# Hybrid encoder layer: a head's outputs spread over more steps with one power for both halves, and the down projection's loads issued one at a time

## The chip, the cores and the metric

The kernel runs on one core of a Trainium2 chip. The metric is the device time of one execution in microseconds (us); of several runs the median counts. Inputs and outputs are float32. The engines are called as in the profile: PE (TensorE, matrix products), PEld (its weight loads), DVE (VectorE), ACT (ScalarE), POOL (GpSimd) and SP (SyncE, which here only issues DMA transfers). Each engine works through its own queue strictly in order; an instruction that waits holds up all that stand behind it on that engine.

## What is computed

One layer on x of 1024 positions by 1024 channels:

```python
h = rmsnorm(x, attn_norm_w)
proj = h @ w_in                      # 1024 x 8192, split into the parts below
glu_in, q, v, z_f, z_b, og, g_a, g_b = split(proj)
a = pointwise(silu(layernorm(dwconv31(glu(glu_in)))))
o = scan(q, v, z_f) + scan_reversed(q, v, z_b)        # 8 heads of 128 columns, chunks
of = o * rsqrt(mean(o * o, axis=-1) + EPS)            # per head, over its 128 columns
bmix = (of * norm_w * silu(og)) @ o_w
x = x + (sigmoid(g_a) * a + sigmoid(g_b) * bmix) @ w_out
h2 = rmsnorm(x, ffn_norm_w)
x = x + (silu(dwconv3(h2 @ w_gate)) * (h2 @ w_up)) @ w_down   # 2816 hidden columns
return rmsnorm(x, final_norm_w)
```

The change touches two places: the line `of = ...` with the multiplication by `silu(og)`, and the product with `w_down`.

## The kernel before

Activations are kept transposed, with channels on the 128 partitions and positions along the row. The 1024 positions are two halves of 512, and a page is a tile of 128 x 512 float32. Each big product is made of three passes over numbers split into a high and a low part: `mm3` issues the matmuls of lines 143, 144 and 145 (128 x 512 each). A split is a cast on ACT (`split`, line 121) and a subtraction on DVE (`split_lo`, line 118); the results are called `hx` or `gx` for activations and `wp` or `wq` for weights.

The order of PE's instructions is the order in which the code issues them. For DVE, ACT, POOL and SP a scheduler orders the instructions when the program is built, by dependencies, by the place in the code and by when it believes that a buffer is free; so a line that stands later in the code may come earlier on such an engine.

To weave two pieces of work on PE, the code writes them as generators. A `Stream` wraps one; `fill(n)` advances it by n steps (fractions are owed, and a negative amount is paid back first), `drain()` runs it out. A step of a job made by `std_job` is two k-blocks, that is six matmuls.

The stage of the heads (about 540 to 990 us) has three pieces of work on PE. `dense` is the rest of the input projection, plain big products. The main loop runs over 8 heads and, inside, two halves: `scan_levels` yields four times (levels 8, 16, 32, 64; products of line 838, for level 8 also line 851; the values v are transposed on line 1034 in the third), then `scan_states` yields three times (two transposes of kG on line 894, each copied by ACT on line 896 into kT, then the products of line 903, whose results go to the states Sf and Sb on lines 909, 911 and 921). After each of these seven steps `between` fills `dense` by 1.3, advances the base of the next half by two steps (DVE work: DE, Qh, Kh, qF, kG, lines 730, 733, 786), and advances `pending` by one. `pending` holds the outputs of the head before. Thus a head's outputs are worked off while the next head's first half is scanned.

`outputs` first finishes Sb (line 989), yields, and hands over to `scan_outputs`. There, before the change, each half in turn is: 11 small matmuls into the bank ob (line 942); a copy into a tm page (944); four squares with a sum over 128 columns each (948); on POOL a scaling and a power of the four sums (`rstd_small`, lines 404 and 405), which gives `ors`; four scalings of the page on ACT (955); a yield. Then for each half: four transposes into a tr bank (963), the product with the norm weight and the gate page (965), and a store to `d_bm`; for the last head a split into `hx` takes the place of the store. The gates are loaded from `d_og` (line 114) into tm pages. There are four tm pages in all, shared with the loads of v and of `d_bm`, two tr banks, one ob bank and three mm banks. Behind the last head `bm_loads` reads `d_bm` back and splits it for the product with `o_w`.

The down projection (from about 1617 us) runs over five groups of 4, 4, 5, 5 and 4 blocks of hidden columns. `load_g` loads the pages of a group from `d_g` (line 1239, three ev pages in turn) and splits them. The pages of the next group are asked for when the current group's stream has made three steps. The result of the first group is copied from the mm bank by ACT (`first_evac`, line 1244, into `xr`), that of the others added on DVE (line 1250).

Of the kernel before, what the change touches and what calls it, by code (L numbers as in the profile page):

```python
# [10 lines left out]
F32 = mybir.dt.float32  # L11
# [3 lines left out]
AF = mybir.ActivationFunctionType  # L15
# [3 lines left out]
P = 128  # L19
# [12 lines left out]
DK = 128  # L32
# [12 lines left out]
def tile_hybrid_encoder(  # L45
# [22 lines left out]
    nc = tc.nc  # L68
    PSUM = bass.MemoryType.PSUM
    V, A, G, T = nc.vector, nc.scalar, nc.gpsimd, nc.tensor  # L70
# [12 lines left out]
    cp = ctx.enter_context(tc.tile_pool(name="const", bufs=1))  # L83
# [7 lines left out]
    def nm(s):  # L91
        uid[0] += 1
        return f"{s}_{uid[0]}"
# [3 lines left out]
    def bank(tag):  # L97
        return ps.tile([P, H], F32, tag=tag, name=nm(tag), bufs=BANKS[tag])

    def page(pool, tag, bufs, dt=F32):  # L100
        return pool.tile([P, H], dt, tag=tag, name=nm(tag), bufs=bufs)

    def tmp():
        return page(mp, "tm", 4)

    def ev():
        return page(mp, "ev", 3)

    def hx():
        return page(mp, "hx", 32, F32R)  # L110

    def load(src):
        t = tmp()
        nc.sync.dma_start(t, src)
        return t
# [4 lines left out]
    def split(hi, lo, src, eng):  # L120
        A.copy(hi, src)  # L121
        split_lo(eng, lo, src, hi)
        return hi, lo
# [25 lines left out]
    def run_jobs(jobs, lead=0, prime=0):  # L149


        jobs = jobs if isinstance(jobs, collections.deque) else collections.deque(jobs)
        ready = collections.deque()

        def prepare(n):
            while jobs and len(ready) < n:
                prep, run = jobs.popleft()
                ready.append((run, prep()))

        prepare(max(prime, 1))  # L160
        if prime:
            yield
        while ready:
            run, w = ready.popleft()
            pieces = run(w)
            for _ in itertools.islice(pieces, lead):
                yield
            prepare(1)
            yield from pieces
            prepare(1)  # L170
# [199 lines left out]
    def vec(key, i):  # L370
        name, o = vec_off[key]
        return vecs[name][:, o + i : o + i + 1]


    def scratch(name, *dims):
        if not dims:
            return dp.tile([P, H], F32, name=name)
        return [scratch(f"{name}_{i}", *dims[1:]) for i in range(dims[0])]
# [8 lines left out]
    d_og = scratch("d_og", NH, 2)  # L387
# [15 lines left out]
    def rstd_small(dst, ss, n):  # L403
        G.tensor_scalar(dst, ss, 1.0 / n, EPS, op0=ALU.mult, op1=ALU.add)
        G.tensor_tensor(dst, dst, mhalf.to_broadcast(list(dst.shape)), op=ALU.pow)
# [257 lines left out]
    for half in range(2):  # L663
# [18 lines left out]
        rs = next(rstd)  # L682
# [32 lines left out]
    dense = Stream(run_jobs(rest_jobs))  # L715


    hp = tc.alloc_tile_pool(name="heads", bufs=1, reuse_waits="tile")
# [207 lines left out]
    def scan_outputs(h, kept, Sf, Sb):  # L926


        ons, gates = [], [load(d_og[h][half]) for half in range(2)]
        for half in range(2):  # L930
            S_t, v, qF = kept[half]
            o = bank("ob")
            for c in range(4):
                sl = slice(c * P, (c + 1) * P)
                g = half * 4 + c
                terms = [(S_t[:, c, :], v[:, c, :])]
                if g > 0:
                    terms.append((qF[:, 1, sl], Sf[half][:, c, :]))
                if g < 7:
                    terms.append((qF[:, 0, sl], Sb[half][:, c, :]))  # L940
                for n, (l, r) in enumerate(terms):
                    T.matmul(o[:, sl], l, r, start=(n == 0), stop=(n == len(terms) - 1))
            on = tmp()
            A.copy(on, o)
            ss = cp.tile([P, 4], F32, name=nm("oss"), tag="oss", bufs=2)
            for c in range(4):
                junk = hp.tile([P, DK], F32, tag="jk", name=nm("jk"), bufs=1)
                A.activation(
                    junk, on[:, c * P : (c + 1) * P], AF.Square, accum_out=ss[:, c : c + 1]
                )  # L950
            rs = cp.tile([P, 4], F32, name=nm("ors"), tag="ors", bufs=2)
            rstd_small(rs, ss, DK)
            for c in range(4):
                sl = slice(c * P, (c + 1) * P)
                A.activation(on[:, sl], on[:, sl], AF.Copy, scale=rs[:, c : c + 1])
            ons.append(on)
            yield
        for half in range(2):
            if half:
                yield  # L960
            b = bank("tr")
            for c in range(4):
                T.transpose(b[:, c * P : (c + 1) * P], ons[half][:, c * P : (c + 1) * P], ident)
            bt = ev()
            V.scalar_tensor_tensor(bt, b, vec("hn", h), gates[half], op0=ALU.mult, op1=ALU.mult)
            if h == NH - 1:
                bm[h][half] = split(hx(), hx(), bt, V)
            else:
                nc.sync.dma_start(d_bm[h][half], bt)
            yield  # L970
# [14 lines left out]
    def outputs(h, kept, Tt, Sf, Sb):  # L985
        for c in range(5, -1, -1):
            hf, cc = c // 4, c % 4
            n1, c1 = (c + 1) // 4, (c + 1) % 4
            V.scalar_tensor_tensor(
                Sb[hf][:, cc, :],  # L990
                Sb[n1][:, c1, :],
                Tt[:, n1, 1, c1 : c1 + 1],
                Sb[hf][:, cc, :],
                op0=ALU.mult,
                op1=ALU.add,
            )
        yield
        yield from scan_outputs(h, kept, Sf, Sb)
# [3 lines left out]
    def bm_loads(half):  # L1002
        for h in range(NH - 1):
            bm[h][half] = split(hx(), hx(), load(d_bm[h][half]), V)
# [5 lines left out]
    pending = Stream(iter(()))  # L1010
    for h in range(NH):
# [31 lines left out]
        pending = Stream(outputs(h, kept, Tt, Sf, Sb))  # L1043
# [2 lines left out]
    pending.fill(1)  # L1046
    dense.fill(left - 20)
    pending.fill(1)
    dense.fill(6)
    pending.fill(1)  # L1050
    dense.fill(6)
    bm_loads(0)
    pending.fill(1)
    dense.fill(8)
# [173 lines left out]
    def g_page():  # L1228
        return hx() if next(n_g) == 0 else page(fd, "gx", 16, F32R)

    groups = [4, 4, 5, 5, 4]
    gs, jobs = [], []

    def load_g(f0, n):
        for f in range(f0, f0 + n):
            gs.append([])
            for half in range(2):
                t = ev()
                nc.sync.dma_start(t, d_g[f][half])
                gs[-1].append(split(g_page(), g_page(), t, V))  # L1240
# [13 lines left out]
    def down_jobs(f0, n, halves, evac):  # L1254
        return [
            std_job(
                w_cols(ffn_w_down, f0 * P, n, i * P),
                n,
                lambda k, half: gs[f0 + k][half],
                evac(i),  # L1260
                halves,
            )
            for i in range(ND)
        ]
# [39 lines left out]
    def finish(half):  # L1304
        turn_out(ND - 1, half)
        ss, y = out_sum[half], out_y[half]
        rs = cp.tile([P, 4], F32, name=nm("frs"), tag="frs", bufs=2)
        V.tensor_reduce(rs, ss.rearrange("p i c -> p c i"), axis=AX.X, op=ALU.add)
        rstd_small(rs, rs, D)
        for c in range(4):  # L1310
            if c % 2:
                A.activation(y[:, c, :], y[:, c, :], AF.Copy, scale=rs[:, c : c + 1])
            else:
                V.tensor_scalar(y[:, c, :], y[:, c, :], rs[:, c : c + 1], None, op0=ALU.mult)
            n = half * 4 + c
            nc.sync.dma_start(out[0, n * P : (n + 1) * P, :], y[:, c, :])
# [4 lines left out]
    f0 = 0  # L1321
# [4 lines left out]
    for n, group in enumerate(groups):  # L1326
        last = n == len(groups) - 1
        for hs in ((0,), (1,)) if last else ((0, 1),):
            st = Stream(run_jobs(down_jobs(f0, group, hs, final_evac if last else add_evac if n else first_evac)))
            st.fill(3)  # L1330
            while late:
                finish(late.pop())
            if not last:
                load_g(f0 + group, groups[n + 1])
            st.drain()
        f0 += group
    finish(late.pop())
# [33 lines left out]
```

## Time and profile before

| what | us |
|---|---|
| median of 3 runs | 1888.44 |
| lowest and highest run | 1885.39, 1894.96 |
| the profiled execution | 1889.98 |
| its span, first to last instruction | 1888.20 |
| busy in the span: PE, DVE, ACT, POOL | 1790.4, 1270.7, 797.8, 212.4 |
| mean granted TensorE clock | 0.982 |

The profile is of one execution. Busy time says how long an engine had at least one instruction at work. In a timeline row the first number is the start in us from the span's beginning, the second the duration, then engine, line, operation, output and input tiles, shape and count; brackets hold the time that the engine stood idle before it and what ended that. In a row of waits the first name waited for the second: total us, number of times, longest. In a row of a stretch the columns are its length, the busy time of PE, PEld, DVE, ACT and POOL with counts, the granted TensorE clock (1.00 is full), the busy share of the DMA engines and GB/s.

### The profile page before, as it was taken

To read this page: it belongs to the slowest core of one execution; us is meant where nothing else is said; L and a number is where in the kernel's file an instruction comes from. 1 tells how busy PE (TensorE), PEld (TensorE's weight loads), DVE (VectorE), ACT (ScalarE), POOL (GpSimd) and SP (SyncE) were. 2 spreads that over 40 slices of the span, in tenths; PEclk is the share of its full clock that TensorE was granted. 3 is DMA by queue.
4 is the path that set the end of the run, shared out by engine and by line. 5 is a ranking of instruction groups with operands and counts; after the bars stand their busy time and mean duration, and the time that the engine had idled before them with its cause. 6 is when DMAs were issued, how large, how long until landed. Compare 5 with 4: busy or idle time off the path is not lost. (4 is left out here: it accounts for less than half of the span.)

```text
span 1888.2 us, 23731 instructions
## 1 busy us (share of the span) xinstructions
PE 1790.4 (95%) x8543; PEld 1477.7 (78%) x8543; DVE 1270.7 (67%) x1860; ACT 797.8 (42%) x1488; POOL 212.4 (11%) x218
## 2 busy tenths in 40 slices
PE   6988999999999999999999999899999999899996
PEld 5767888877788887888877888678888888788885
DVE  3488999535469898999936555766676666534445
ACT  6333343234555555665443134544343434522124
POOL 3101111213100001000000000211111111000000
PEclk8999999999999999999999999999999999999998
DMA  7747788776562333332228665777676665733125
GB/s 261 221 118 169 182 195 195 180 180 159 185 200 85 117 97 106 112 110 81 82 69 251 193 197 174 178 159 154 145 156 147 146 148 129 218 96 95 55 85 167
DMA packets 322764, 282.99 MB, mean 150 GB/s; under 512 B 14798, under 2 KB 244950, under 8 KB 322646
## 3 DMA queue, kind: packets, MB, share of 16 engines
q1 hardware_dynamic: 270854, 240.57, 41.1%
q0 software_dynamic: 51792, 40.90, 15.3%
q8 instruction: 67, 1.10, 0.2%
q14 instruction: 51, 0.42, 0.1%
HBM read 189.14 MB, written 71.83 MB: 138 GB/s over the span
## 5 line engine op out<-in xcount | busy, mean ns | idle before, releaser
L143 PE MATMUL mm<-hx,wp 128*128 128x512 f32 x1176 | 481.1, 409 | 21.9 <-ACT xr L1244 4.8
L145 PE MATMUL mm<-hx,wp 128*128 128x512 f32 x1176 | 466.6, 397 | 4.6 <-DVE wp L118 4.6
L144 PE MATMUL mm<-hx,wp 128*128 128x512 f32 x1176 | 466.5, 397 | 2.1 <-POOL hx L118 1.9
L121 ACT CAST wp<-wr 128x1024 fp32r<-128x1024 f32 (+2 forms) x196 | 179.6, 917 | 337.9 <-PE mm L144 203.7
L118 DVE TENSOR_TENSOR wp<-wr,wp 128x1024 fp32r<-128x1024 f32 (+2 forms) x196 | 207.0, 1056 | 119.9 <-ACT wp L121 114.3
L143 PEld LDWEIGHTS mm<-hx,wp 128*128 128x128 f32 x1176 | 225.7, 192 | 72.2 <-ACT su L266 5.8
L145 PEld LDWEIGHTS mm<-hx,wp 128*128 128x128 f32 x1176 | 225.1, 191 | 55.7 <-DVE wp L118 6.7
L144 PEld LDWEIGHTS mm<-hx,wp 128*128 128x128 f32 x1176 | 225.7, 192 | 47.7 <-POOL hx L118 3.6
L645 DVE SCALAR_TENSOR_TENSOR acc<-gl,v_b,acc 128x1024 f32<-128x1024 f32 x120 | 149.1, 1277 | 0.5
L238 POOL DMA_DIRECT2D wr<-sw x39 | 34.9, 895 | 512.9 <-DVE wp L118 251.9
L1250 DVE TENSOR_TENSOR xr<-mm,xr 128x512 f32<-128x512 f32 x48 | 33.2, 691 | 82.0 <-PE mm L145 81.9
L838 PEld LDWEIGHTS sc<-qF,A 128*128 128x128 f32 x512 | 65.3, 192 | 19.1 <-issue 13.3
L838 PE MATMUL sc<-qF,A 128*128 128x128 f32 x512 | 68.2, 276 | 11.7 <-DVE qF L730 10.6
L121 ACT CAST wq<-sw 128x1024 fp32r<-128x1024 f32 x39 | 41.0, 1051 | 80.0 <-PE mm L144 62.8
L143 PE MATMUL mm<-hy,wp 128*128 128x512 f32 x156 | 62.2, 399 | 8.9 <-ACT wp L121 5.9
L835 ACT COPY A<-kG 128x512 f32<-128x512 f32 x64 | 39.7, 621 | 66.6 <-DVE kG L730 38.0
L1172 DVE SCALAR_TENSOR_TENSOR tm<-gp,v_a,tm 128x512 f32<-128x512 f32 x88 | 65.6, 746 | 1.7 <-ACT tm L1168 0.9
L266 ACT COPY su<-mm 128x512 f32<-128x512 f32 x78 | 45.4, 581 | 48.7 <-PE mm L145 48.5
L144 PE MATMUL mm<-hy,wp 128*128 128x512 f32 x156 | 61.8, 396 | 0.0
L145 PE MATMUL mm<-hy,wp 128*128 128x512 f32 x156 | 61.3, 393 | 0.0
L143 PE MATMUL tr<-hx,wp 128*128 128x512 f32 x156 | 61.2, 392 | 0.0
L143 PE MATMUL sc<-hy,wq 128*128 128x512 f32 x156 | 61.1, 392 | 0.0
(289 smaller groups left out, 3602.1 us busy)
## 6 DMA issues: line engine op xcount, KB each, us to landing
wr<-in_w_in_dram SPq DMA_DIRECT2D x55, 512.0 KB, 6.6
sw<-in_ffn_w_up_dram SPq DMA_DIRECT2D x44, 256.0 KB, 4.1
sw<-in_ffn_w_up_dram POOLq DMA_DIRECT2D x22, 512.0 KB, 8.5
wr<-in_ffn_w_up_dram SPq DMA_DIRECT2D x22, 512.0 KB, 4.9
d_g<-ft SPq DMA_DIRECT2D x44, 256.0 KB, 5.9
ev<-d_g SPq DMA_DIRECT2D x44, 256.0 KB, 3.1
wr<-sw POOLq DMA_DIRECT2D x39, 256.0 KB, 3.3
wr<-wr POOLq DMA_DIRECT2D x39, 256.0 KB, 4.4
```

The lines of the kernel that those rows point to most:

```text
L118: eng.tensor_tensor(lo, src, hi.bitcast(F32), op=ALU.subtract)
L121: A.copy(hi, src)
L143: T.matmul(acc, whi[:, k, :], ahi, start=first, stop=False, skip_group_check=again)
L144: T.matmul(acc, whi[:, k, :], alo, start=False, stop=False, skip_group_check=again)
L145: T.matmul(acc, wlo[:, k, :], ahi, start=False, stop=last, skip_group_check=again)
L238: G.dma_start(o, a, accum_op=ALU.add)
L266: A.copy(t, acc)
L645: V.scalar_tensor_tensor(acc, g[:, k : k + S], tap(k), acc, op0=ALU.mult, op1=ALU.add)
L835: A.copy(A_t.rearrange("p (b x e) -> p b x e", x=2, e=h), pairs(kG, h))
L838: T.matmul(b[:, c * P : (c + 1) * P].rearrange("p (b x e) -> p b x e", x=2, e=h), A_t[:, c * P : (c + 1) * P], view(qF, c * P, [[2 * h, P ...
L1172: V.scalar_tensor_tensor(c, g[:, o + k : o + k + H], vec("fdw", k * NF + j), c, op0=ALU.mult, op1=ALU.add,)
L1250: V.tensor_tensor(xr[i][half], acc, xr[i][half], op=ALU.add)
```

## The change

In `scan_outputs`, the sums of squares and their powers of both halves get one tile each of 2 x 4 columns, and `rstd_small` runs once for both. Gates get pages of their own (tag og, two buffers). The steps are: matmuls, copy and squares of half 0; the same for half 1 and the power; an empty step; scaling of half 0; scaling of half 1; transposes and gate of half 0; of half 1. With the step for Sb these are eight, where before there were six, one of them empty, so that the last falls into the next head's second half. Behind the last head, three fills of `dense` by 4 with steps of `pending` between them take the place of two by 6.

In the down projection, the stream of a group is advanced by nine further steps, and then the next group's blocks are loaded one by one with four steps between them.

```diff
     def scan_outputs(h, kept, Sf, Sb):
-        ons, gates = [], [load(d_og[h][half]) for half in range(2)]
+        ons, gates = [], []
+        ss = cp.tile([P, 2, 4], F32, name=nm("oss"), tag="oss", bufs=2)
+        rs = cp.tile([P, 2, 4], F32, name=nm("ors"), tag="ors", bufs=2)
         for half in range(2):
...
             on = tmp()
             A.copy(on, o)
-            ss = cp.tile([P, 4], F32, name=nm("oss"), tag="oss", bufs=2)
             for c in range(4):
                 junk = hp.tile([P, DK], F32, tag="jk", name=nm("jk"), bufs=1)
                 A.activation(
-                    junk, on[:, c * P : (c + 1) * P], AF.Square, accum_out=ss[:, c : c + 1]
+                    junk, on[:, c * P : (c + 1) * P], AF.Square, accum_out=ss[:, half, c : c + 1]
                 )
-            rs = cp.tile([P, 4], F32, name=nm("ors"), tag="ors", bufs=2)
-            rstd_small(rs, ss, DK)
+            ons.append(on)
+            gates.append(page(hp, "og", 2))
+            nc.sync.dma_start(gates[half], d_og[h][half])
+            if half == 0:
+                yield
+        rstd_small(rs, ss, DK)
+        yield
+        yield
+        for half in range(2):
             for c in range(4):
                 sl = slice(c * P, (c + 1) * P)
-                A.activation(on[:, sl], on[:, sl], AF.Copy, scale=rs[:, c : c + 1])
-            ons.append(on)
+                A.activation(
+                    ons[half][:, sl], ons[half][:, sl], AF.Copy, scale=rs[:, half, c : c + 1]
+                )
             yield
         for half in range(2):
-            if half:
-                yield
             b = bank("tr")
...
     dense.fill(left - 20)
     pending.fill(1)
-    dense.fill(6)
-    pending.fill(1)
-    dense.fill(6)
+    dense.fill(4)
+    pending.fill(2)
+    dense.fill(4)
+    pending.fill(2)
+    dense.fill(4)
     bm_loads(0)
...
             if not last:
-                load_g(f0 + group, groups[n + 1])
+                st.fill(9)
+                for f in range(f0 + group, f0 + group + groups[n + 1]):
+                    load_g(f, 1)
+                    st.fill(4)
             st.drain()
```

## The prediction

> **What bounds the kernel now.** I read the page's first two parts, then stretches of the span, then the waits of PE, ACT and DVE inside the stretches that the diff touches, then the timeline.
>
> ```profile
> PE 1790.4 (95%) x8543; PEld 1477.7 (78%) x8543; DVE 1270.7 (67%) x1860; ACT 797.8 (42%) x1488; POOL 212.4 (11%) x218
> ...
> 700.00:750.00 50.00, 46.21 (x283) 39.44 (x282) 43.06 (x80) 28.46 (x66) 6.39 (x4) 0.97 0.33 105
> ...
> 800.00:850.00 50.00, 47.84 (x307) 42.08 (x306) 47.55 (x88) 29.11 (x67) 2.40 (x4) 1.00 0.34 106
> ...
> 632.00:634.00 2.00, 2.00 (x6) 1.57 (x5) 0.00 (x0) 1.63 (x5) 0.34 (x1) 0.50 0.90 331
> ```
>
> PE is the bound, with 98 us idle in the span. From 540 to 990 us, the stage of the heads, its busy times add up to 420.8 of 450 us, so 29 us are to be had; DVE stands at 43 to 48 of each 50 us there, so it binds next. In the last row PE ran at half its clock just after a stall.
>
> ```profile
> PE sc L838 <- DVE qF L730: 10.6, 9, 2.8
> PE tr L894 <- ACT kT L896: 7.4, 3, 2.9
> PE tr L894 <- DVE ev L965: 4.0, 3, 1.8
> PE tr L963 <- ACT tm L955: 1.9, 2, 1.5
> ...
> ACT tm L955 <- POOL ors L405: 26.8, 16, 4.0
> ...
> DVE kG L730 <- ACT A L835: 12.5, 6, 3.7
> ```
>
> These are waits (total us, times, longest) of the stage, the DVE row from 600 to 950. PE's second, third and fourth rows are the head's outputs: ACT stands still for POOL's power, everything queued on ACT is late, and both PE and DVE pay. One head, in time (start, us, what, idle before):
>
> ```profile
> 727.93 2.87 POOL L404 TENSOR_SCALAR ors<-oss 128x4 f32<-128x4 f32 x1 [43.69 <-ACT jk L948]
> 730.89 1.42 POOL L405 TENSOR_TENSOR ors<-ors,mhalf 128x4 f32<-128x4 f32 x1
> 732.34 1.28 ACT L955 ACTIVATE tm<-tm,ors 128x128 f32<-128x128 f32 x4 [3.97 <-POOL ors L405]
> 732.79 1.21 PE L963 MATMUL tr<-ident,tm 128*128 128x128 f32 x4 [1.49 <-ACT tm L955]
> 743.36 0.69 DVE L730 TENSOR_TENSOR kG<-kG,tb 128x512 f32<-128x512 f32 x1 [3.73 <-ACT A L835]
> 743.86 1.16 PE L903 MATMUL sc<-v,kT 128*128 128x128 f32 x8 [0.77 <-ACT kT L896]
> ```
>
> And the start of the down projection, where the first bank's copy stands behind casts of loads that are not yet needed:
>
> ```profile
> 1627.59 0.62 ACT L121 CAST hx<-ev 128x512 fp32r<-128x512 f32 x1 [1.93 <-DMA ev<-d_g]
> 1629.41 0.62 ACT L121 CAST hx<-ev 128x512 fp32r<-128x512 f32 x1 [1.20 <-DMA ev<-d_g]
> 1629.93 0.58 ACT L1244 COPY xr<-mm 128x512 f32<-128x512 f32 x1
> 1630.56 0.80 PE L143 MATMUL mm<-hx,wp 128*128 128x512 f32 x1 [4.79 <-ACT xr L1244]
> ```
>
> **Instructions.** The order of PE's instructions is the same in both kernels but for the two output transposes (L963) of heads 0 to 6: before, they stand ahead of the first L894 and ahead of L903; after, half 0's stands 6 or 12 big matmuls behind L903 and half 1's behind the next half's first levels. Eight L404 and eight L405 go, 16 POOL instructions. ACT, DVE and SP keep their work; d_og's 16 loads (256 KB, 2.8 us to landing) get pages of their own and two of the four tm pages come free. POOL's 212 us carry nothing on the chain: what its saving is worth is the wait on ACT alone.
>
> **Worth of a half-clock stretch.** After the 2.89 us stall at 631 us ten big matmuls start 3.96 us apart in all (631.44 to 635.40) where 0.23 us each is usual: 1.6 us lost. The stage has three more-than-1.4-us stalls of the outputs followed by this (631, 733, 946 us). The Trainium skill (TensorE: Matmul & The Clock Gate, "HAM oscillation — how this bites in real kernels") says that a gap must pass about 3.4 us before the clock is halved; gaps of 2.89 and 2.55 us were enough here, so the trace decides, and by the page's rule 1.6 us for each would have to be left out.
>
> **Step 1, outputs of heads 0 to 6.** I lay ACT's new order over the old moments. Head 2: half 1's output matmuls end at 728.9 and the squares of half 0 at 726.9 as before. Behind them now come L752 and L753 twice each (0.52 each), L755 (0.8), the copy of half 1 (0.56), L755 (0.8), four squares (0.43) between two L873 (0.35), one L591 (0.55): 734.0; kT (0.5), wp (0.95): 735.5; the power is ready at 736.0; scale of half 0 (1.2), second kT (0.55): 737.8; scale of half 1 (1.2); A at 739.0. PE, without a transpose between, reaches the second L903 at 737.0, waits 0.8, and ends it at 738.7; before, it ended at 744.9. Less the two transposes still owed (0.9) PE is 5.3 us ahead. DVE's kG starts at 739.7, not 743.36, and DVE ends the Sf updates and one of two L965 at 742.8, not both at 747.7: less 0.75, 4.2 us ahead. The L894 wait disappears since its bank is now freed by the early v copy; the wait that takes its place is L903's on the second kT, behind the one power and one scale. In the same way, heads 0 to 6 in turn: PE 3.7, 1.6, 5.3, 0.8, 0.6, 1.2, 5.1, in all 18.3 us; DVE 1.1, 0.4, 4.2, 0.0, -0.3, 0.6, 3.4, in all 9.4 us. In heads 1, 3, 4 and 5 both scales now stand ahead of an A copy or of f, and DVE gets back what it gained. PE meets DVE once a head (L838 waits for qF, 0.5 to 1.4 us, before), so an earlier PE waits there longer: I take DVE's figure, **9 us**, with 0 and 18 as the ends. The cover of the edit is the big matmuls: 6 or 12 of 0.23 us stand between each step; gone, the wait is the power and two scales, 3.9 us a head.
>
> How long the power takes is the size I trust least. The pair L404 and L405 took 1.2 to 4.3 us; half 0's eight 2.2 in the mean, half 1's eight 1.4, and the one kept falls where half 1's fell. I take 1.4. The Trainium skill (SBUF — State Buffer, "Who interferes with whom") says that a GpSimd instruction that reads SBUF is blocked by a VectorE instruction with two SBUF inputs. The trace agrees: the 4.00 us power at 935.8 lies under two such products (0.68 and 1.22 us) and a subtraction, the 1.01 us ones under the reciprocal.
>
> **Step 2, last head.** Half 1's matmuls end at 983.7, then 12 big matmuls (2.8 us) and the transpose of half 0, which stood ready at 986.5. Now it needs half 1's copy and squares (to 986.2), the power (1.4) and a scale (1.28): 988.9, a stall of 2.4 us and perhaps one half-clock stretch: 2.4 to 4.0 lost. Late next are L965 and the hx splits behind it on DVE, 11 us before they are used. Against it, at 1003.2 PE waits 1.9 + 0.2 us for the casts of d_bm, whose loads stood behind gates in the tm pages and behind a store on SP; two pages are free now and the loads stand ahead of that store. With the half clock seen after it, 3.8 us. Together **0.2 us lost**, between 4 lost and 3.8 won.
>
> **Step 3, down projection.** The loads dealt out are still hoisted by the scheduler: in the new order seven of the eight casts of group 1 stand ahead of the first xr copy; one moved behind. So the copy starts at 1628.2, not 1629.93, and the stall falls from 4.8 to 3.1 us. After 4.8 us the half clock lasted about 6.8 us, after 2.9 us half of that: 1.6 more. **3.3 us** won; the ends are 0 and 8.0 (4.8 + two stretches, no stall left). Later groups have no PE wait to lose: from 1700 to 1850 PE is busy in every 50 us whole. A load's 3.1 us and two splits (1.3) fit between the matmuls of the four yields (5.5 us) that follow it; were they late, each would cost at most these 4.4 us.
>
> Sum: 9 - 0.2 + 3.3 = 12.1 us. The profiled execution took 1889.98 us (span 1888.20), so 1877.9; it lies 1.5 us above the median 1888.44, on whose scale this is 1876.4, rounded to **1877 us**.
>
> **Rivals.** (B) DVE sets the pace of the stage and only the lengthened powers of heads 2 and 6 mattered by chance: heads 0, 1, 3, 4, 5 give 1.8 us on DVE, the down stage its 1.7 without a clock stretch, the last head takes 0.2 to 2: about **1886**. For it: DVE's 47.55 of 50 us; against: DVE's idle in 600 to 950 is nearly all waits for ACT. (C) PE is not held by DVE and keeps its 18.3 us: 1888.4 - 18.3 - 3.3 + 0.2 = **1867**. For it: three half-clock stretches go with the stalls; against: the nine qF waits. (D) The other side: the single power now gates both halves, and behind its scale on ACT stand the second kT, f and A. If it falls under DVE's two-input products and takes 4.2 us, each of seven heads loses 2.8 us more (19), three stalls reach the 2.9 us that halved the clock (5), the last head 3: 12.1 - 27 gives **1903**. It decides from a mean pair of about 3.0 us, where 7.5 times the excess over 1.4 eats the 12.1. For it: 4.29 and 4.19 among 16 pairs; against: both are half 0's. (E) The down edit does nothing at all: 1880, inside the forecast.
>
> **Chances.** Forecast 0.47 (own range 1870 to 1883), B 0.23, C 0.17, D 0.13. The range 1864 to 1893 leaves out D and the far end of C. Runs of before differ by 0.5%, about what can be told from no change: below 1879.0 lie C and three quarters of the forecast, 0.52; within, B and the rest, 0.35; slower, D, 0.13.
>
> **What would show it.** ACT's wait for ors: eight, under 10 us in all. L894 without waits; L903 with about 0.5 to 1 us a head. DVE's wait for A below 8 us. One half-clock stretch fewer at 632, 735 and 946 us each. PE's stall at the first xr copy near 3 us, and 2.4 us ahead of the last head's first transpose. Power pairs above 3 us, or qF waits grown by 10 us, would make it wrong.

## Result and profile after

| | before | after |
|---|---|---|
| median of 15 runs each, us | 1888.44 | 1883.05 |
| lowest to highest, us | 1884.84 to 1897.29 | 1874.37 to 1886.90 |
| profiled execution, us | 1889.98 | 1885.96 |
| its span, us | 1888.20 | 1884.20 |

The ratio after to before is 0.9962, 95% interval 0.9949 to 0.9975: of 1888.4 us, 7.2 us are gone, between 4.7 and 9.6. The forecast was 12.1 us on the profiled execution. That pair differs by 4.0 us.

The page's busy times and the same stretches of the changed kernel (length, busy time of PE, PEld, DVE, ACT and POOL, granted clock, DMA share, GB/s):

```profile
PE 1790.5 (95%) x8543; PEld 1478.6 (78%) x8543; DVE 1270.1 (67%) x1860; ACT 797.2 (42%) x1488; POOL 198.0 (11%) x202
```

```profile
700.00:750.00 50.00, 46.95 (x307) 41.77 (x308) 47.77 (x89) 28.44 (x67) 2.51 (x2) 1.00 0.35 106
...
632.00:634.00 2.00, 1.27 (x10) 1.22 (x11) 0.00 (x0) 2.00 (x7) 0.00 (x0) 1.00 0.00 0
```

From 700 to 750 us PE issues 307 instructions where it issued 283, at a full clock (0.97 before): the work is the same and is done sooner. At 632 us, where PE ran at half its clock, the clock is 1.00. POOL's busy time falls by 14 us.

Waits of the heads' stage after (540 to 990 us, the DVE row 600 to 950: total us, times, longest):

```profile
PE sc L838 <- DVE qF L730: 13.2, 11, 2.8
PE sc L903 <- ACT kT L896: 5.4, 6, 1.3
PE tr L970 <- ACT tm L963: 2.1, 1, 2.1
PE sc L851 <- ACT Sb L921: 1.8, 2, 1.5
...
ACT tm L963 <- POOL ors L405: 11.2, 8, 2.0
...
DVE kG L730 <- ACT A L835: 7.0, 4, 2.6
```

Both rows of L894 (7.4 and 4.0 us) are gone. In their place stands L903's wait for the second kT, and PE waits more often for DVE's qF (13.2 against 10.6 us). ACT waits for the power eight times, not sixteen, and 11.2 us, not 26.8; DVE's wait for A falls from 12.5 to 7.0 us. The same head as before the change, in time:

```profile
730.97 0.88 POOL L404 TENSOR_SCALAR ors<-oss 128x8 f32<-128x8 f32 x1 [48.40 <-ACT jk L949]
731.93 1.63 POOL L405 TENSOR_TENSOR ors<-ors,mhalf 128x8 f32<-128x8 f32 x1
...
733.59 1.28 ACT L963 ACTIVATE tm<-tm,ors 128x128 f32<-128x128 f32 x4 [1.29 <-POOL ors L405]
...
734.78 0.56 ACT L896 COPY kT<-tr 128x512 f32<-128x512 f32 x1
735.25 1.28 ACT L963 ACTIVATE tm<-tm,ors 128x128 f32<-128x128 f32 x4
...
735.40 1.16 PE L903 MATMUL sc<-v,kT 128*128 128x128 f32 x8 [0.66 <-ACT kT L896]
737.06 0.69 DVE L730 TENSOR_TENSOR kG<-kG,tb 128x512 f32<-128x512 f32 x1 [1.84 <-ACT A L835]
```

The power still holds ACT for 1.29 us, but PE no longer waits for the scales themselves: between the two groups of L903 it waits 0.66 us for a kT copy that stands behind one of them on ACT. L903 runs at 735.4, before at 743.9.

Three places of the changed kernel behind that stage (start us, us, what, idle before):

```profile
976.64 1.63 POOL L405 TENSOR_TENSOR ors<-ors,mhalf 128x8 f32<-128x8 f32 x1
978.31 2.45 ACT L963 ACTIVATE tm<-tm,ors 128x128 f32<-128x128 f32 x8 [2.03 <-POOL ors L405]
...
978.77 1.35 PE L970 MATMUL tr<-ident,tm 128*128 128x128 f32 x4 [2.12 <-ACT tm L963]
...
1087.02 0.69 DVE L1077 TENSOR_TENSOR tm<-tm,tm 128x512 f32<-128x512 f32 x1 [3.04 <-DMA tm<-d_a]
1088.47 0.62 ACT L121 CAST mg<-tm 128x512 fp32r<-128x512 f32 x1 [5.82 <-DVE tm L1079]
...
1089.14 0.49 PE L143 MATMUL mm<-mg,wp 128*128 128x512 f32 x1 [3.05 <-ACT mg L121]
...
1623.71 0.62 ACT L121 CAST hx<-ev 128x512 fp32r<-128x512 f32 x1 [1.86 <-DMA ev<-d_g]
...
1624.87 0.80 PE L143 MATMUL mm<-hx,wp 128*128 128x512 f32 x1 [3.29 <-ACT xr L1253]
```

The last head's first transposes wait 2.12 us for the shared power. At w_out's start PE waits 3.05 us for the last merged page (before: 0.58), which comes out of a chain: a load of d_a, two DVE instructions, a cast, and a page that comes free for a further load. And the first xr copy of the down projection keeps PE for 3.29 us (before: 4.79).

**Where the time went, by stage.** Three stretches, each between two events that every kernel here has: from the first v copy of head 0 to the last kT copy of head 7 (heads); from there to the first matmul of the FFN's statistics, L420 (last head's outputs, o-projection, merge, w_out); from there to the end of the span (FFN, down). The times are those of one profiled execution each; the kernels below other than before and after are described with their experiments.

| kernel | first v copy at | heads | to the FFN | rest | span |
|---|---|---|---|---|---|
| before | 571.5 | 400.5 | 209.0 | 707.2 | 1888.2 |
| after | 572.5 | 389.5 | 212.8 | 709.4 | 1884.2 |
| heads' part only (e1) | 566.9 | 387.9 | 216.9 | 703.3 | 1875.0 |
| down part only (e2) | 570.0 | 397.5 | 210.2 | 704.2 | 1881.9 |
| + d_a in ev pages (e3) | 571.0 | 389.7 | 212.1 | 705.3 | 1878.1 |
| + casts on DVE (e4) | 574.3 | 388.9 | 215.0 | 702.6 | 1880.8 |
| before + gate pages (e5) | 568.0 | 399.0 | 208.5 | 708.3 | 1883.8 |
| one power, old steps (e6) | 569.7 | 430.1 | 214.3 | 702.9 | 1917.0 |
| spread, two powers (e7) | 571.5 | 395.3 | 209.0 | 704.2 | 1880.0 |
| e3 and e4 together (e8) | 571.1 | 387.8 | 210.7 | 703.2 | 1872.8 |
| e8, two powers at last head (e9) | 571.7 | 387.8 | 211.4 | 702.8 | 1873.7 |
| e9, three steps (e10) | 573.2 | 389.8 | 215.9 | 702.8 | 1881.7 |
| e8, loads as before (e11) | 566.5 | 388.6 | 211.5 | 701.4 | 1868.0 |

The first column is a warning: the change doesn't touch PE's order ahead of it, and it still spreads over 7.8 us. So a single pair of profiles cannot tell 4 from 8 us, but kernels that share a stage can be pooled. In before and after the four differences are +1.0, -11.0, +3.8 and +2.2, in sum -4.0.

### The profile page after: what moved, and what is told of

It reads as the page before. It is cut to its first block, busy times and chain, and to the rows that moved or that the text cites. A ratio compares the mean times of both kernels' runs of the same rounds, so it can differ in the third digit from the quotient of the medians.

```text
span 1884.2 us, 23705 instructions
## 1 busy us (share of the span) xinstructions
PE 1790.5 (95%) x8543; PEld 1478.6 (78%) x8543; DVE 1270.1 (67%) x1860; ACT 797.2 (42%) x1488; POOL 198.0 (11%) x202
## 4 chain that ended last, share of the span: by engine, by line
PE 48%; DVE 21%; DMA 18%; ACT 6%; issue 4%; POOL 2%; SPq 0%; ACTq 0%; DVEq 0%; POOLq 0%
PE mm L143 12%; PE mm L144 12%; PE mm L145 12%; DMA wr<-wr 3%; DMA tm<-d_a 3%; DVE wp L118 2%; DMA wr<-sw 2%; PE sc L143 2%; PE sc L145 2%; PE sc L144 2%; DVE kG L730 2%; DMA sw<-in_w_in_dram 2%; DVE acc L645 2%; DMA wr<-in_w_in_dram 2%; DVE qF L730 2%
## 5 line engine op out<-in xcount | busy, mean ns | idle before, releaser
L838 PE MATMUL sc<-qF,A 128*128 128x128 f32 x512 | 68.8, 277 | 13.8 <-DVE qF L730 13.2
```

What stands on the lines that cost most here:

```text
L838: T.matmul(b[:, c * P : (c + 1) * P].rearrange("p (b x e) -> p b x e", x=2, e=h), A_t[:, c * P : (c + 1) * P], view(qF, c * P, [[2 * h, P ...
```

## Experiments

All eleven were timed in five rounds beside the kernel before. Ratios are to it.

**e1: the heads' part alone.** The down projection is that of before:

```diff
             if not last:
-                st.fill(9)
-                for f in range(f0 + group, f0 + group + groups[n + 1]):
-                    load_g(f, 1)
-                    st.fill(4)
+                load_g(f0 + group, groups[n + 1])
```

> Only the heads' part of the change (outputs spread, one power, gates in own pages); the down projection's loads are as before. Theory (the heads' stage wins about 10 us, of which 2.3 are lost at the last head and 2 to 4 given back where the w_out product waits for the merged pages and where the FFN starts): end 4 to 6 us earlier than before, ratio 0.9968 to 0.998; the wait of w_out's first matmul for ACT's mg near 3 us as in the full change. Rival 1 (the forecast's sum, nothing given back): 8 to 9 us, ratio 0.9955. Rival 2 (the full change's gain is mostly the down part or chance): under 2 us, ratio above 0.999.

Measured: 0.9964 (0.9946 to 0.9983), 1881.32 us: 6.8 us. The wait for mg is 3.2 us. The small-gain rival is out, as its 0.999 lies outside the interval. The time itself lies between the theory and the forecast's 0.9955, and both stay inside the interval; the stretches tell them apart: heads 387.9 against 400.5 us, then 216.9 against 209.0. The gain of the heads is real and part of it is given back behind them.

**e2: the down part alone**, the reverse edit.

> Only the down projection's part (loads dealt out singly); the heads are as before. Theory (the stall at the first xr copy shrinks from 4.8 to 3.3 us, the half-clock stretches around it stay): 1.5 us won, ratio 0.9992. The forecast's sum: 3.3 us, ratio 0.9983, with one half-clock stretch fewer. Rival (nothing): 1.000, stall near 4.8 us.

Measured: 0.9989 (0.9969 to 1.0008), 1885.71 us. PE waited 4.10 us at the first xr copy, with one half-clock stretch behind it. The time does not separate 0 from 3.3 us. Whatever the down part is worth, it is the smaller one.

**e3: room for the merge's loads.**

```diff
-            sb, sa, a = load(d_gb[i][half]), load(d_ga[i][half]), load(d_a[i][half])
+            sb, sa, a = load(d_gb[i][half]), load(d_ga[i][half]), ev()
+            nc.sync.dma_start(a, d_a[i][half])
```

> The changed kernel, with one of the three loads of each merge (that of d_a) in the three ev pages rather than in the four tm pages, so that loads run further ahead. Theory (the gain of the heads is given back at the merge because its 16 loads go one after another through the tm pages): the wait of w_out's first matmul for mg falls from 3.0 to under 1 us, the stage before w_out ends 2 to 3 us earlier, ratio against before 0.994 to 0.996 (0.9962 without this edit), or less where the FFN's start then waits longer for its weights (3.9 us). Rival (TensorE itself sets the pace there): wait gone but w_out starts when it did; ratio 0.996.

Measured: 0.9951 (0.9934 to 0.9968), 1878.37 us. PE has no wait for mg left, and the stretch to the FFN takes 212.1 us where the changed kernel, e1 and e4, all with the old merge, took 212.8, 216.9 and 215.0. (e7, below, has the old merge too and took 209.0; it is taken up under step 2.) The time is on the theory's side, though the rival's 0.996 lies inside the interval, and the intervals of this kernel and of the changed one overlap.

**e4: casts of the second group on DVE.**

```diff
-                gs[-1].append(split(g_page(), g_page(), t, V))
+                hi, lo = g_page(), g_page()
+                (V.tensor_copy if groups[0] <= f < groups[0] + groups[1] else A.copy)(hi, t)
+                split_lo(V, lo, t, hi)
+                gs[-1].append((hi, lo))
```

> The changed kernel, with the eight casts of the down projection's second group on DVE rather than ACT, so that no cast for a page still on its way stands ahead of the first xr copy on ACT. Theory (those casts are what the first xr copies wait for): the stall of 3.3 us falls under 1 us and the half-clock stretch of 6.8 us behind it (worth half of it, 3.4 us) goes: 3 to 6.5 us, ratio against before 0.993 to 0.9946. Rival 1 (the stretch is not tied to this stall): stall gone, stretch stays, ratio 0.9945. Rival 2 (what is late is a page of the first group or a weight, not the copy): TensorE waits as long, on another thing, ratio 0.996; DVE's own queue then shows the loads' lateness.

Measured: 0.9951 (0.9933 to 0.9969), 1879.24 us. The one stall of 3.29 us becomes three of 1.69, 0.68 and 0.50 us, and the clock stays at 1.00 from 1618 to 1630 us. So the casts were what the copies stood behind, and in this execution no half clock followed. 2.9 us of waits are left, so the stall did not go below 1 us as the theory had it: the copy that keeps PE for 1.69 us stands behind a cast again, one of the third group (gx, on ACT at 1628.46 us behind its load).

**e5: the gates' pages alone**, added to the kernel before:

```diff
-        ons, gates = [], [load(d_og[h][half]) for half in range(2)]
+        ons, gates = [], []
...
             ons.append(on)
+            gates.append(page(hp, "og", 2))
+            nc.sync.dma_start(gates[half], d_og[h][half])
             yield
```

> The kernel before, with the gate tiles alone loaded into two pages of their own; a power for each half, the old steps, the old down projection. Theory (only the spreading takes TensorE's waits away): the waits of the kT transposes (L894's 7.4 + 4.0 us before) stay, 540 to 990 us shows about 30 us of waits of TensorE, ratio 0.998 to 1.002. Rival (the four tm pages, of which two were held by gates from the first step, were what made the outputs late): those waits fall to under 5 us and the ratio to 0.997.

Measured: 0.9999 (0.9977 to 1.0020), 1885.41 us. The three rows in question have the totals of before (total us, times, longest):

```profile
PE tr L894 <- ACT kT L896: 7.4, 3, 2.9
PE tr L894 <- DVE ev L967: 4.0, 3, 1.7
...
ACT tm L955 <- POOL ors L405: 26.8, 16, 4.0
```

Where the gates lie is worth nothing by itself.

**e6: one power, in the old steps.** Products of each half, then power and all eight scales in the second half's step, then one step for each half's transposes:

```diff
         rstd_small(rs, ss, DK)
-        yield
-        yield
         for half in range(2):
...
-            yield
+        yield
         for half in range(2):
             b = bank("tr")
```

> The changed kernel, with one power for both halves and the gates in own pages, but worked off in the old number of steps: products of each half, then power and all scales in the second half's step, then one step for each half's transposes. Theory (it is the spreading that wins; one power in itself only puts 1.64 us plus eight scales ahead of the first transposes): TensorE's wait for the scales comes back or grows, 10 us or more at L970 or at the kT transposes; the heads' stage is no shorter than before, ratio (with the down part's 1.5 us) 0.998 to 1.002. Rival (one power fewer a head and its shared-port waits are the gain): 0.9962 as in the full change.

Measured: 1.0165 (1.0140 to 1.0190), 1918.73 us: 31 us slower, far more than either side expected. Its waits from 570 to 1030 us, and one head in time:

```profile
PE tr L968 <- ACT tm L961: 42.2, 8, 7.4
```

```profile
627.84 1.64 POOL L405 TENSOR_TENSOR ors<-ors,mhalf 128x8 f32<-128x8 f32 x1
...
629.52 2.45 ACT L961 ACTIVATE tm<-tm,ors 128x128 f32<-128x128 f32 x8 [1.54 <-POOL ors L405]
...
629.97 1.35 PE L968 MATMUL tr<-ident,tm 128*128 128x128 f32 x4 [5.54 <-ACT tm L961]
```

Every head now stops PE for some 5 us while half 1's copy, its squares, the power and the first scale pass one after another. The clock pays too: the granted clock from 570 to 1000 us is 0.95, and the heads take 430.1 us, 31 more than the 399.0 of the mean of before, e2 and e5. One power is no gain in itself: once both halves wait for one power, the steps between it and the transposes are needed. Whether the gain is made of these steps is another question; the times by head under step 1 bear on it.

**e7: the steps, with two powers.**

```diff
+            rstd_small(rs[:, half], ss[:, half], DK)
             if half == 0:
                 yield
-        rstd_small(rs, ss, DK)
         yield
         yield
```

> The changed kernel, with a power for each half again (128x4, right after its squares), all else as changed. Theory (the power is off TensorE's path once the steps are spread): heads 0 to 6 as in the change; at the last head the first transposes wait about 0.6 us less (a 128x4 power is 1.0 us, a 128x8 one 1.64 us): ratio 0.996. Rival (sharing the power is part of the gain, through eight powers of GpSimd that stand in DVE's way and it in theirs): 1 to 4 us longer, ratio 0.997 to 0.9985.

Measured: 0.9968 (0.9949 to 0.9986), 1881.48 us, not to be told from the change. The last head's wait at L970 is gone altogether. But one power took 6.06 us and ACT stood for it (rows of head 1):

```profile
673.75 6.06 POOL L405 TENSOR_TENSOR ors<-ors,mhalf 128x4 f32<-128x4 f32 x1
674.19 1.22 DVE L730 TENSOR_TENSOR qF<-Qh,fm 128x1024 f32<-128x1024 f32 x1
675.32 1.22 DVE L730 TENSOR_TENSOR kG<-Kh,DE 128x1024 f32<-128x1024 f32 x1
...
679.35 1.76 DVE L786 RECIPROCAL DE<-DE 128x256 f32<-128x256 f32 x1
679.84 1.28 ACT L963 ACTIVATE tm<-tm,ors 128x128 f32<-128x128 f32 x4 [7.05 <-POOL ors L405]
```

It ends when DVE's unbroken run of products has given way to the reciprocal. PE then waited 3.6 us once for kT, and the heads took 395.3 us against 389.5. From the last kT copy of head 1 to that of head 2, while head 1's outputs are worked off, e7 took 58.47 us and the changed kernel 52.79: nearly the whole difference lies in this head. So the spread steps do not cover a power as long as this one. The shared power may help, not by the eight powers that go but by where it falls: in the changed kernel all eight took 1.63 to 1.65 us, six of them begun under the reciprocal. The timing does not separate the two.

**e8: e3 and e4 together.**

> The changed kernel with both edits that won 2 us each by themselves: d_a in the ev pages, and the second group's casts on DVE. Theory (they lie in different stages and add): 4 us under the changed kernel, ratio against before 0.994; no wait of w_out for mg, the longest wait at the first xr copies under 2 us, no half-clock stretch near 1630 us. Rival (what one stage wins is given back at the FFN's start, where the weights' loads set the time): 0.995 to 0.996.

Measured: 0.9912 (0.9889 to 0.9935), 1871.56 us, 16.6 us faster than before (0.88% of 1886.1) and faster than the changed kernel, whose interval ends at 0.9949. Its waits from 985 to 1220 us, and the longest at the first xr copies:

```profile
PE mm L143 <- ACT su L266: 4.0, 1, 4.0
PE sc L412 <- ACT tm L411: 3.1, 2, 1.8
PE mm L145 <- DVE wp L118: 2.3, 1, 2.3
```

```profile
1623.68 0.50 PE L143 MATMUL mm<-hx,wp 128*128 128x512 f32 x1 [0.73 <-ACT xr L1257]
```

No mg in the list and 0.73 us at xr. The rival (given back at the FFN's start) is out. The wait of 4.0 us at the FFN's start remains, as in the changed kernel (3.9). But the theory's ratio missed as well: 0.994 lies above the interval. Apart, e3 and e4 each stand 0.0011 below the changed kernel's ratio, about 2 us; together 0.0050, about 9 us. The three stretches differ from the changed kernel's by -1.7, -2.1 and -6.2 us; why the two edits are worth more than their sum is open.

**e9: e8 with a power for each half at the last head alone.**

```diff
+            if h == NH - 1:
+                rstd_small(rs[:, half], ss[:, half], DK)
             if half == 0:
                 yield
-        rstd_small(rs, ss, DK)
+        if h < NH - 1:
+            rstd_small(rs, ss, DK)
```

> The kernel of the last comparison (changed kernel, d_a in the ev pages, second group's casts on DVE: 0.9912), with a power for each half at the last head alone. Theory (the last head's 2.1 us before its first transposes are the wait for the shared power, and with the merge's loads running ahead a gain there is kept): that wait under 0.7 us, 1 to 3 us won, ratio 0.990. Rival (the loads of the merge set the time there): the wait goes and turns up at w_out's first matmul, ratio 0.991.

Measured: 0.9920 (0.9899 to 0.9940), 1874.17 us. The wait goes and nothing is seen to be won: the stretch to the FFN takes 211.4 us against 210.7. But nothing turned up at mg, where the rival looked for it. The waits from 985 to 1220 us show one for the weights' split in four pieces where e8 had one (2.3 us):

```profile
PE mm L145 <- DVE wp L118: 5.3, 4, 2.7
PE mm L143 <- ACT su L266: 3.3, 1, 3.3
```

e11, without this edit, has 4.2 us of the first row too, so it can't be put down to the edit, and where the 2.1 us went stays open.

**e10: e9 with a third step between power and scales.**

```diff
         yield
         yield
+        yield
         for half in range(2):
```

> As e9, with three steps rather than two between the power and the scales of heads 0 to 6. Theory (the 5.3 us that TensorE waits for the second kT come from scales, with their wait for the power, that stand ahead of that copy on ACT): where the scales now come behind the copy, the wait goes; 2 to 4 of the 5.3 us and of ACT's 11 us for ors are won, ratio 0.989. Rival (another thing of the same moment, DVE's kG, sets the pace): L903's wait moves to the products with A and qF, ratio as e9.

Measured: 0.9961 (0.9946 to 0.9975), 1879.35 us, slower than e9, which neither side expected. L903's waits fell only from 5.3 to 4.4 us (the scheduler still put scales ahead of the kT copy in some heads). The edit adds the step at the last head too, so all outputs end later, and PE met a new wait that ended at 1003.8 us (row of 985 to 1220):

```profile
PE mm L143 <- ACT hx L121: 8.8, 2, 8.7
```

Those are the casts of d_bm that the o-projection starts with, and the casts waited for the loads of d_bm. That the later outputs put these loads late is likely, but not shown. Of the two numbers tried, two steps are the better.

**e11: e8 with the down projection's loads issued as before.**

> The kernel of 0.9912 with the down projection's loads issued together as before the change, the second group's casts still on DVE. Theory (what stands ahead of the xr copies on ACT is the lever, not when loads are issued): waits at the first xr copies under 2 us, ratio 0.991. Rival (dealing out the loads is worth its own 1.5 us and more once the casts are gone): ratio 0.992 to 0.993, waits at the xr copies over 2 us.

Measured: 0.9914 (0.9894 to 0.9934), 1871.14 us, with 0.43 us at the first xr copy. With the casts off ACT it makes no difference that can be told when the loads are issued.

## Why the prediction came out as it did

The direction and the largest term were right; the sum was 12.1 us and 7.2 (4.7 to 9.6) came. The single time 1877 lay 6 us under the median of 1883.05. That median is inside the stated range of 1864 to 1893, but a hair above the forecast's own 1870 to 1883, and nearer to rival B's 1886; more chance (0.52) had been given to times below 1879.0 than to those from there on (0.35). So the total alone does not choose between the forecast and B. The stretches have to.

**Step 1 (9 us): right in size and in place.** Pooling kernels with the same outputs, the heads took 399.0 us before (mean of 400.5, 397.5, 399.0) and 388.7 after (mean of after, e1, e3, e4, e8, e11): 10.3 us. PE's idle time in the stretch falls from 23.6 to 18.0 us in the mean of the same kernels; the other 4.6 us are busy time that the same matmuls no longer need, about what three half-clock stretches cost at the 1.6 us of the prediction. By head, from the last kT copy (L896) of one head to that of the next, in us:

| outputs of head | 0 | 1 | 2 | 3 | 4 | 5 | 6 |
|---|---|---|---|---|---|---|---|
| before, e2, e5 (mean) | 52.97 | 53.97 | 54.49 | 51.42 | 50.12 | 50.68 | 54.68 |
| after, e1, e3, e4, e8, e11 (mean) | 51.61 | 52.81 | 50.21 | 52.87 | 50.01 | 50.59 | 50.00 |
| won | 1.4 | 1.2 | 4.3 | -1.4 | 0.1 | 0.1 | 4.7 |
| forecast, DVE's | 1.1 | 0.4 | 4.2 | 0.0 | -0.3 | 0.6 | 3.4 |

The forecast by DVE is met within 1.5 us in every head, so choosing it over PE's 18.3 was right. The reason given for the choice is borne out only in part: the waits for qF grew by 2.6 us, a third of what lies between 18.3 and 10.3. L903's waits were 0.92, 0.64, 0.66, 1.29, 0.75 and 1.11 us where 0.5 to 1 a head were forecast; L894 is free, DVE's wait for A is below 8 us, and the half-clock stretches at 632, 735 and 946 us are gone. A new one came up at 801 us, behind a wait of 1.93 us for qF; head 3 took some 52.3 us without it and 53.95 with it. The power pair was mis-sized (1.4 us against 1.9 in the mean), as was ACT's wait (under 10 us against 11.2); what PE pays for that is part of L903's 5.4 us.

The table also says what the gain hangs on, and there the prediction told only half. 9.0 of the 10.2 us lie in heads 2 and 6, and these are the two whose power pair was long before (4.29 and 4.19 us). It was long in the profiles of e2 and e5 too (4.2 to 4.3 us each), so it is no chance of one execution, as rival B had it, but a steady cost of the old order. The other five heads won 1.3 us in all. In e7, with the new steps, heads 2 and 6 had powers of 1.01 to 1.39 us and were as short as in the changed kernel (50.42 and 49.61 us), while the one power of 6.06 us cost head 1 5.7 us in spite of the steps. So most of the gain seems to come from power pairs that no longer fall under a run of DVE's products, and little from the steps as a cover. This is argued from heads set side by side; no run moves the power and keeps the steps. That the steps are needed once the power is shared is shown by e6: without them each head's transposes wait 5.3 us (42.2 in eight), not the 3.9 of the prediction, as half 1's copy and squares stand in the chain too, and the clock adds to it. Rival D's lengthened power exists (6.06 us in e7), but in the changed kernel none was lengthened.

**Step 2 (0.2 us lost): this is the step that failed.** The stall was right (2.12 us against 2.4, and the matmuls behind it started 0.43 us apart where 0.23 is usual, for 2.5 us). The wait of 1.9 + 0.2 us for d_bm vanished, too (but e5, with the old outputs, did not have it either). The step booked that as a gain to be kept. It looked for what comes late next in the hx splits, 11 us before their use, and not at the loads behind them: the 16 loads of d_a go one after another through the four tm pages, and that chain set the start of w_out. DVE's waits of 985 to 1100 us, before and in the changed kernel:

```profile
DVE tm L1068 <- DMA tm<-d_a: 22.8, 15, 3.2
```

```profile
DVE tm L1077 <- DMA tm<-d_a: 26.1, 16, 3.3
```

The chain was there before the change: 15 of the 16 were waited for. PE was late enough then to wait only 0.58 us for its end; it now arrives earlier and waits 2.8 to 3.2 us (after, e1, e4), and not at all with d_a in other pages (e3). Pooled, the stretch from the last kT copy to the FFN took 209.2 us before (209.0, 210.2, 208.5) and 214.9 after (212.8, 216.9, 215.0): 5.7 us given back, not 0.2. e7 has the old chain as well and gave nothing back here (209.0), but its heads ended later: heads and this stretch together took 602.3, 604.8, 603.9 and 604.3 us in after, e1, e4 and e7, so heads that differ by up to 7.4 us moved the end of this stretch by 2.5 us at most. With d_a in other pages it took 211.4 (212.1, 210.7, 211.5, of e3, e8 and e11), so by these means 3.5 of the 5.7 are that chain; the single stretches spread by up to 4 us, so that figure is rough. The rest has the size of the last head's stall, but e9, which takes this stall away, was not seen to win; what holds the last 2.2 us is open.

**Step 3 (3.3 us): right in kind, its size not settled.** The stall shrank from 4.79, 4.39 and 5.51 us (before, e1, e5) to 3.29, 4.10, 2.77 and 3.29 (after, e2, e3, e7): 1.5 us in the mean, where 1.7 were worked out. The half-clock stretch that was to go was gone in two of those four kernels and shorter in one, but not in the changed kernel's profiled execution. The timings give e2 0.9989 with an interval across 1, and the rest of the span differs by 0.5 us (706.3 against 705.8, means of the same kernels). That seven of eight casts still stood ahead, which the prediction saw and did not act on, was the point: e4, e8 and e11 move them, and the rest takes 702.4 us in the mean, 3.4 less again.

The three pooled terms are -10.3, +5.7 and -0.5, in sum 5.1 us won, inside the timed interval. That the sum came no lower owes something to luck: the heads won 1.3 us more than was booked, which made up for a part of the 5.5 us that step 2 lost beyond its 0.2 and the 2.8 that step 3 fell short. Rivals: C (PE keeps 18.3, 1867) is out by the heads' 10.3 us. B (1886) had the other five heads right (1.8 us, measured 1.3) and is out in that the long powers of heads 2 and 6 stand in every profile of the old order, and their 9.0 us are won. D did not happen, and E (the down edit does nothing) can't be told from the forecast.

## What to carry to other kernels

Look head by head before saying what a gain is made of: here 9.0 of 10.2 us came from the two heads in which a small GpSimd instruction lay under a run of VectorE products. When two such chains are merged, put independent steps between them and the engine that binds; merged without those steps, the same edit cost 31 us. Ahead of booking the gain, follow the stage behind it to the next meeting of the engines: if loads go one by one through a few pages there, an engine that arrives earlier just waits for them, and other pages for a third of those loads brought back some 3.5 of 5.7 us here. And before spreading loads out, look at what stands in the queue ahead of the copy that is late: moving the casts to another engine did what moving the loads could not.

## What was not expected of the hardware

The clock is not tied to a stall's length alone. At the first xr copy the changed kernel and e7 both stalled 3.29 us. These are the 10 us from there in each (PE's clock is the third number from the end):

```profile
1624.00:1634.00 10.00, 9.13 (x28) 7.34 (x29) 4.31 (x7) 5.98 (x12) 0.00 (x0) 0.67 0.91 296
```

```profile
1621.00:1631.00 10.00, 8.61 (x38) 7.14 (x39) 4.02 (x7) 6.09 (x11) 0.00 (x0) 1.00 0.88 306
```

The changed kernel (first) was halved, e7 (second) was not; 2.77 us (e3) did not halve it either, 2.65 us (e6, at 1658 us) did. In the heads of the changed kernel 1.93 us (at 800 us) halved it and 1.96 us (at 748 us) did not. The Trainium skill (TensorE: Matmul & The Clock Gate, "HAM oscillation — how this bites in real kernels") gives gaps over about 3.4 us as what must be avoided; these runs show no such border: gaps of 1.9 to 3.3 us went either way, and what decides it is open. A forecast that books such a stretch as won books too much.

A GpSimd power of 128x4 took 1.01 us under DVE's reciprocal and 6.06 us under a run of its products. The Trainium skill (SBUF — State Buffer, "Who interferes with whom") has the two engines share a port pair as an exclusive lock, and the trace agrees in these two; beyond that, the wait lasted through some ten DVE instructions in a row. It does not come about each time: in the kernel before, powers of 1.01 us at 782.34 and 833.30 us lie under such a product, and not under the reciprocal as the prediction has it for all of 1.01 us.
